# One SBUF tile for all slabs, with slabs 1 and 2 loaded by one DMA and slabs 4 and 5 stored by one DMA

## Chip, cores, metric

One core of one Trainium2 chip. The metric is device time in microseconds of that core; lower is better. Some runs fall over 1.5% above the fastest of the same kernel; these are left out of every ratio.

## The reference

Rotary embedding with split heads, on 16 x 512 x 1024 float32 (33.55 MB in, 33.55 MB out):

```python
x = x.reshape(batch, seq, num_heads, head_dim)       # 16, 512, 16, 64
x1, x2 = x[..., :half_dim], x[..., half_dim:]
rotated = np.concatenate([x1 * cos - x2 * sin,
                          x1 * sin + x2 * cos], axis=-1)
```

## The kernel before

The input is cut into eight slabs of two batch entries. A slab is 4 MB: 128 partitions with one row of 32 KB each. Five slabs are held in SBUF at a time, so load 5 waits until store 0 has landed, load 6 for store 1, load 7 for store 2. Loads are issued from SP, stores from ACT.

```python
slots = 5
slabs = ctx.enter_context(tc.tile_pool(name="slabs", bufs=slots))
xpool = ctx.enter_context(tc.tile_pool(name="xpool", bufs=2))

def dram(t, s, a=0, n=W):
    return bass.AP(tensor=t.tensor, offset=t.offset + s * nb * seq * dim + a,
                   ap=[[W, P], [1, n]])

def load(s):
    slab[s] = slabs.tile([P, W], f32, tag="slab", name="slab")
    return nc.sync.dma_start(out=slab[s], in_=dram(x, s))

load(0)
# ... the cos and sin tables are loaded ...
for s in range(1, slots):
    load(s)
# ... tables spread over 128 partitions by four matmuls ...

# passes: slab 0 in two halves, slabs 1 to 5 whole, slabs 6 and 7 in two halves
cast(passes[0])                               # ScalarE: float32 slab -> bf16 xb
for i, (s, r, n) in enumerate(passes):
    if i + 1 < len(passes):
        cast(passes[i + 1])
    # ... xs, xu: this pass's part of slab[s] and xb[s]; t2: bf16 view of slab[s]
    for t, a in ((t2, rpp * hd), (xu, 0)):    # VectorE: two products
        nc.vector.tensor_mul(out=t, in0=xu, in1=view(tab, ...))
    nc.vector.tensor_add(out=xu, in0=xu, in1=view(t2, ...))   # VectorE: the sum
    nc.scalar.copy(out=xs, in_=xu)            # ScalarE: copy back, bf16 -> float32
    if r + n == rpp:
        nc.scalar.dma_start(out=dram(out_flat, s), in_=slab[s])
        if s + slots < nslabs:
            load(s + slots)
```

The framework inserts all semaphores, and at build time it also orders the instructions of each engine. The source's order is a proposal: in the trace of before, slab 1's cast (L110) stands ahead of both copies of slab 0 (L137), while the source has it between them.

## Time and profile before

| | before |
|---|---|
| time, median of 3 | 162.0 us |
| span of the profiled run | 160.2 us |
| ScalarE busy, VectorE busy | 113.6 us (71%), 108.4 us (68%) |
| DMA: bytes, rate over the span | 67.24 MB, 420 GB/s |

Instructions are named by engine and source line; a bracket gives the idle time before one and what ended it. A q behind an engine's name stands for its sequencer, which issues instructions and DMAs.

### The profile page before, as it was taken

The page shows a single profiled execution, that of the slowest core. Times are in us where ns is not written, and L with a number is a line of the kernel's source. Part 1 is how long each engine was busy: PE and PEld are TensorE (multiplying, and loading weights), DVE is VectorE, ACT ScalarE, POOL GpSimd, SP SyncE. Part 2 cuts the span into 40 slices and gives each one's busy share as a digit, 9 for nine tenths or more (in the row PEclk, how much of TensorE's full clock was granted, in tenths as well). Part 3 has the DMA queues.
Part 4 walks back from the last instruction along what each step waited for, and adds up shares of the span by engine and source line. Part 5 has one row for each costly group of instructions (what it writes and reads, how often), then busy time and mean ns, then how long its engine had stood idle before and what let it go on. Part 6 is the DMA issues. An engine that isn't in the chain of part 4 may idle for free.

```text
span 160.2 us, 157 instructions
## 1 busy us (share of the span) xinstructions
PE 1.2 (1%) x4; PEld 0.5 (0%) x4; DVE 108.4 (68%) x34; ACT 113.6 (71%) x23; POOL 1.8 (1%) x9
## 2 busy tenths in 40 slices
PE   0001100000000000000000000000000000000000
PEld 0000000000000000000000000000000000000000
DVE  0000399999999996997999499939569599900000
ACT  3005939998959899989969995199995999280000
POOL 2000000000000000000000000000000000000000
DMA  7999999999999999999999999999999999999993
GB/s 237 425 401 409 393 458 458 393 425 483 401 393 507 409 393 475 434 401 442 458 409 425 475 409 401 499 409 393 491 425 393 458 450 401 425 475 409 401 499 147
DMA packets 2464, 67.24 MB, mean 420 GB/s; under 512 B 288, under 2 KB 416, under 8 KB 416
## 3 DMA queue, kind: packets, MB, share of 16 engines
q1 hardware_dynamic: 1152, 33.55, 49.3%
q10 hardware_dynamic: 1312, 33.69, 48.8%
HBM read 33.69 MB, written 33.55 MB: 420 GB/s over the span
## 4 chain that ended last, share of the span: by engine, by line
DMA 41%; ACT 21%; DVE 20%; issue 6%; PE 0%; POOLq 0%; POOL 0%; ACTq 0%; DVEq 0%; SPq 0%
DMA out_dram<-slab 19%; DMA slab<-in_x_dram 15%; ACT slab L137 13%; ACT xb L110 8%; DMA cos_sb<-in_cos_dram 7%; DVE xb L131 7%; DVE slab L131 7%; DVE xb L134 6%; DVE tab L101 1%; PE acc L95 0%; POOLq L172 0%; POOL tab L90 0%; ACTq L139 0%; DVEq L131 0%; SPq L62 0%
## 5 line engine op out<-in xcount | busy, mean ns | idle before, releaser
L110 ACT CAST xb<-slab 128x4096 bf16<-128x4096 f32 (+1 forms) x11 | 56.6, 5155 | 23.5 <-DMA slab<-in_x_dram 22.2
L137 ACT CAST slab<-xb 128x4096 f32<-128x4096 bf16 (+1 forms) x11 | 56.6, 5153 | 5.2 <-DVE xb L134 5.2
L131 DVE TENSOR_TENSOR slab<-xb,tab 128x4096 bf16<-128x4096 bf16 (+1 forms) x11 | 35.9, 3260 | 12.8 <-ACT xb L110 12.7
L131 DVE TENSOR_TENSOR xb<-xb,tab 128x4096 bf16<-128x4096 bf16 (+1 forms) x11 | 35.9, 3261 | 0.3
L134 DVE TENSOR_TENSOR xb<-xb,slab 128x4096 bf16<-128x4096 bf16 (+1 forms) x11 | 35.9, 3260 | 0.3
L101 DVE CAST tab<-acc 128x1024 bf16<-128x1024 f32 x1 | 1.2, 1224 | 18.7 <-PE acc L95 18.7
L110 ACT ACT_TABLE_LOAD x1 | 1.3, 1283 | 2.0 <-issue 2.0
L95 PE MATMUL acc<-tab,pick 64*128 64x256 bf16 x4 | 1.2, 392 | 17.5 <-POOL tab L90 17.5
L83 POOL TENSOR_SCALAR_AFFINE_SELECT pick<-pick 64x128 bf16<-64x128 bf16 x2 | 0.5, 287 | 0.1
L90 POOL CAST tab<-cos_sb 64x256 bf16<-64x256 f32 x1 | 0.4, 389 | 10.6 <-DMA cos_sb<-in_cos_dram 10.6
L95 PEld LDWEIGHTS <-pick 64*128 64x128 bf16 x4 | 0.5, 113 | 17.7 <-issue 16.2
L90 POOL CAST tab<-sin_sb 64x256 bf16<-64x256 f32 x1 | 0.4, 394 | 4.9 <-DMA sin_sb<-in_sin_dram 4.9
L80 POOL MEMSET pick<- 64x256 bf16 x1 | 0.3, 305 | 0.3 <-POOLq L158 0.3
L158 POOL MEMSET const-bfloat16-1.0<- 128x1 bf16 x1 | 0.1, 106 | 0.0
L158 POOL MEMSET const-uint8-127<- 128x1 uint8 x1 | 0.1, 106 | 0.0
L158 POOL MEMSET const-float32-0.0<- 128x1 f32 x1 | 0.1, 103 | 0.2 <-issue 0.2
L158 POOL MEMSET const-float32-1.0<- 128x1 f32 x1 | 0.1, 103 | 0.0
## 6 DMA issues: line engine op xcount, KB each, us to landing
slab<-in_x_dram SPq DMA_DIRECT2D x8, 4096.0 KB, 24.2
out_dram<-slab ACTq DMA_DIRECT2D x8, 4096.0 KB, 25.6
cos_sb<-in_cos_dram ACTq DMA_DIRECT2D x1, 64.0 KB, 11.5
sin_sb<-in_sin_dram ACTq DMA_DIRECT2D x1, 64.0 KB, 16.2
```

The source lines that it names most:

```text
L80: nc.gpsimd.memset(pick, 0.0)
L83: nc.gpsimd.affine_select(out=part, in_=part, compare_op=mybir.AluOpType.not_equal, fill=1.0 - 2.0 * g, base=0, pattern=[[0, P // SP], [-1 ...
L90: nc.gpsimd.tensor_copy(out=view(tab1, i * TW, (1, TW)), in_=t)
L95: nc.tensor.matmul(view(acc, i * rpp * hd + h * half, (hd, rpp), (1, half)), view(pick, i * h * P, (1, P)), view(tab1, i * TW, (half, rpp) ...
L101: nc.vector.tensor_copy(out=tab, in_=acc)
L110: nc.scalar.copy(out=view(xb[s], r * dim, (1, n * dim)), in_=view(slab[s], r * dim, (1, n * dim)))
L131: nc.vector.tensor_mul(out=t, in0=xu, in1=view(tab, a + r * hd, (hd, n), (0, nh), (1, hd)))
L134: nc.vector.tensor_add(out=xu, in0=xu, in1=view(t2, half, (hd, n * nh), (-half, 2), (1, half)))
L137: nc.scalar.copy(out=xs, in_=xu)
L158: nc = _bacc.Bacc("TRN2", target_bir_lowering=False, num_devices=1)
```

## The change

The intent is fewer and larger DMAs: 18 become 16. A persistent tile of five places replaces the pool. Slab s sits at place (s + 1) % 5, which puts 1 beside 2 and 4 beside 5. No compute operation changes.

```diff
-    slabs = ctx.enter_context(tc.tile_pool(name="slabs", bufs=slots))
+    mem = singles.tile([P, slots * W], f32, tag="mem")
+
+    def at(s):
+        return (s + 1) % slots * W
+
+    def dram(t, s, n):
+        return bass.AP(tensor=t.tensor, offset=t.offset + s * nb * seq * dim,
+                       ap=[[W, P], [nb * seq * dim, n], [1, W]])
+
+    def sbuf(s, n):
+        return view(mem, at(s), (W, n), (1, W))
+
+    def load(s, n=1):
+        nc.sync.dma_start(out=sbuf(s, n), in_=dram(x, s, n))
...
-    for s in range(1, slots):
+    load(1, 2)
+    for s in range(3, slots):
         load(s)
...
-            nc.scalar.dma_start(out=dram(out_flat, s), in_=slab[s])
+            if s != 4:
+                first, count = (4, 2) if s == 5 else (s, 1)
+                nc.scalar.dma_start(out=dram(out_flat, first, count),
+                                    in_=sbuf(first, count))
```

(Cut: the compute lines, where slab[s] becomes a view of mem at at(s).)

More of the change, by code (lines that the diff above doesn't have):

```diff
@@ L44 @@
         name="psum", bufs=1, space=bass.MemoryType.PSUM))
-    def dram(t, s, a=0, n=W):
-        return bass.AP(tensor=t.tensor, offset=t.offset + s * nb * seq * dim + a,
-                       ap=[[W, P], [1, n]])
     def view(t, offset, *dims):
@@ L54, in view @@
                                    ap=[t.ap[0], *[list(d) for d in dims]])
-    slab = {}
-    def load(s):
-        slab[s] = slabs.tile([P, W], f32, tag="slab", name="slab")
-        return nc.sync.dma_start(out=slab[s], in_=dram(x, s))
+    mem = singles.tile([P, slots * W], f32, tag="mem")
[8 more added lines that the diff above has]
+        nc.sync.dma_start(out=sbuf(s, n), in_=dram(x, s, n))
     load(0)
@@ L110, in cast @@
         nc.scalar.copy(out=view(xb[s], r * dim, (1, n * dim)),
-                       in_=view(slab[s], r * dim, (1, n * dim)))
+                       in_=view(mem, at(s) + r * dim, (1, n * dim)))
     passes = []
@@ L125 @@
             cast(passes[i + 1])
-        xs = view(slab[s], r * dim, (1, n * dim))
+        xs = view(mem, at(s) + r * dim, (1, n * dim))
         xu = view(xb[s], r * dim, (1, n * dim))
-        t2 = view(slab[s].bitcast(bf16), 2 * r * dim, (1, n * dim))
+        t2 = view(mem.bitcast(bf16), 2 * (at(s) + r * dim), (1, n * dim))
         for t, a in ((t2, rpp * hd), (xu, 0)):
```

## The prediction

> **What bounds the kernel now.** I read the page first: busy shares, the 40 slices, the queues.
>
> ```profile
> PE 1.2 (1%) x4; PEld 0.5 (0%) x4; DVE 108.4 (68%) x34; ACT 113.6 (71%) x23; POOL 1.8 (1%) x9
> ...
> DMA  7999999999999999999999999999999999999993
> GB/s 237 425 401 409 393 458 458 393 425 483 401 393 507 409 393 475 434 401 442 458 409 425 475 409 401 499 409 393 491 425 393 458 450 401 425 475 409 401 499 147
> DMA packets 2464, 67.24 MB, mean 420 GB/s; under 512 B 288, under 2 KB 416, under 8 KB 416
> ...
> q1 hardware_dynamic: 1152, 33.55, 49.3%
> q10 hardware_dynamic: 1312, 33.69, 48.8%
> ```
>
> No compute engine is above 71%, but the DMA row is 9 from the second slice to the last but one: the 16 DMA engines are the bound. A table by windows shows how full they are in each kind of traffic (loads alone, loads and stores, stores alone):
>
> ```profile
> core 0: us, PE busy (x) PEld busy (x) DVE busy (x) ACT busy (x) POOL busy (x), PEclk, DMA share, GB/s
> 2.00:37.00 35.00, 1.16 (x4) 0.35 (x3) 18.18 (x8) 21.73 (x6) 0.78 (x2) 1.00 0.97 412
> 38.00:120.00 82.00, 0.00 (x0) 0.00 (x0) 70.94 (x19) 72.26 (x12) 0.00 (x0) 1.00 1.01 434
> 125.00:155.00 30.00, 0.00 (x0) 0.00 (x0) 13.76 (x6) 15.79 (x5) 0.00 (x0) 1.00 1.01 435
> ```
>
> The share is 1.01 in the last two. Every byte counts, and 67.24 MB at some 430 GB/s is 156 us; the rest of the 160.2 us is the start before the first byte (about 1.5 us), the small table packets, and the last landing. So the bytes are unchanged by the diff, and the only things that can move the time are the rate and *idle time of the DMA engines*. The rest of this text asks whether the queues ever run dry.
>
> The timeline gives the times at which work is put in the queues:
>
> ```profile
> 23.63 7.02 ACT L110 CAST xb<-slab 128x8192 bf16<-128x8192 f32 x1 [2.80 <-DMA slab<-in_x_dram]
> ...
> 30.56 7.11 ACT L137 CAST slab<-xb 128x4096 f32<-128x4096 bf16 x2
> ...
> 33.44 4.42 DVE L131 TENSOR_TENSOR slab<-xb,tab 128x8192 bf16<-128x8192 bf16 x1
> ...
> 37.70 0.35 ACTq L139 DMA_DIRECT2D out_dram<-slab  x1
> ...
> 53.86 0.34 ACTq L139 DMA_DIRECT2D out_dram<-slab  x1
> ...
> 98.21 0.34 ACTq L139 DMA_DIRECT2D out_dram<-slab  x1
> ...
> 114.15 0.34 ACTq L139 DMA_DIRECT2D out_dram<-slab  x1
> ...
> 144.28 0.34 ACTq L139 DMA_DIRECT2D out_dram<-slab  x1
> ```
>
> Stores 0, 1, 4, 5 and 7 in that order. The reader sees that slab 1 is cast the moment it lands (23.63), before slab 0's copies back at 30.56, and that the VectorE goes straight from slab 0 to slab 1 at 33.44.
>
> **What the Trainium skill says.** "DMA: Bandwidth & Descriptors", section "Why a DMA increments its semaphore by 16 and not by 1": only the full count means that all data landed. So in one DMA of two slabs, slab 1 can't be used before slab 2 is there too. Nothing in the trace of before has such a DMA, so this is the premise. "SBUF — State Buffer", section "The DMA setup-cost knee (why "@ 1 MiB" ≠ asymptote)": a transfer pays about 2 us that doesn't scale with bytes, mostly completion latency; coalescing is advised. The trace differs for queued transfers: 4 MB DMAs behind one another already run at 434 to 435 GB/s, so that latency is hidden here and there is nothing for coalescing to win. "Perfetto Trace Analysis", section "DMA Optimizations": splitting may let work start sooner. This change does the reverse; the trace agrees in that the cast of slab 1 waits for its DMA (2.80 us).
>
> **The change part by part.**
> (1) It removes one load and one store issue. Issues take 0.33 to 0.65 us on their queues, beside transfers; 4 MB still goes in 128 rows of 32 KB. Each DMA has 1152/8 = 144 packets, 128 of data and 16 small ones. Taking 2 x 16 small ones away is worth under 0.1 us.
> (2) The single tile keeps five places of 32 KB a partition: slabs 5, 6, 7 take those of slabs 0, 1, 2 as before, and load 5 still waits for store 0 to land, load 6 for store 1, load 7 for store 2. The compute instructions keep shapes and counts (casts 7.02 us, VectorE 4.42 us): 0.
> (3) Slab 1 comes later. Slab 1 landed at 23.63; another 4.19 MB at 432 GB/s (the rate in 20 to 37 us) is 9.7 us, so slabs 1 and 2 land at 33.3. ACT casts slab 1 then. Store 0 stays bound by the VectorE (the tables arrive late, slab 0 is done at 33.5). In the source, ACT's order is copy back of slab 0's first half, cast of slab 1, copy back of the second half, store 0. I take that as the middle case: cast 33.3 to 40.3, copy to 43.9, store 0 at 43.9 (6 us later). VectorE on slab 1: 40.4 to 53.7 (7 us later than at 33.44); copy back 53.7 to 60.7; store 1 at 60.8 (before 53.86).
> Do the queues run dry before that? Until store 1, the work is loads 0 to 4, the tables and store 0: 5 x 4.19 + 0.13 + 4.19 = 25.30 MB. The trace of before has moved 24.77 MB by 60 us; the remaining 0.53 MB takes 1.2 us, so that work is used up at 61.2. Store 0 ends it and lands about 1.5 us later, so load 5 is issued at 62.5 or so; store 1, issued at 60.8, has bytes 1.0 us later (as load 0: issued 0.74, first packets at about 1.7), at 61.8. Idle: 0.6 us.
> (4) Store 4 is held for slab 5. Before, it sat in the queue from 98.21, but the store queue reached it only near 120: by then loads (33.5 MB) are in, and what is left, 160.2 less 120 at 434 GB/s, is about four stores. In the middle case store 1 at 60.8, 14.35 us per slab (54.24 to 68.59, cast to cast): store 2 at 75.1, store 3 at 89.5, cast of slab 5 to 96.5, VectorE to 109.8, copy 116.8, the double store at 116.9. Walking both queues with half the rate each (9.7 us a slab alone, 19.3 shared), store 2 ends at 99, store 3 at 118. So the double store is there, just, and load 7 runs to about 120 as well. Idle: 0. Afterwards stores 4 to 7 are 38.7 us, and store 7 is needed at about 150, against 144.28 before and some 146 now: 4 us of slack.
> Sum: -0.1 + 0 + 0.6 + 0 = +0.5 us in the middle case.
>
> **The rivals.**
> *A: the scheduler puts both copies back before slab 1's cast.* Then store 0 stays at 37.7, but the cast is 37.2 to 44.2, VectorE to 57.5, store 1 at 64.6. Store 0 lands at 61.0 as before and load 5 has bytes at 62: idle 0.8 us. All later stores are 3.8 us later than in the middle case: store 3 at 93.2, VectorE on slab 5 ends at 113.5, the double store at 120.6 with bytes at 121.6; store 3 ends at 117.4 and load 7 at 119.9. Idle 1.7 more. Sum +2.5: 164.5 us. Speaking for it: ACT is idle and those copies are ready at about the same time as the data.
> *B: the order of before stays, slab 1's cast ahead of both copies.* Cast 33.3 to 40.3, copies to 47.4, store 0 at 47.5, cast of slab 2, copy, store 1 at 61.7, bytes at 62.7: idle 1.5 us, the double store at 117.8 in time. 163.5 us. For it: the trace of before has this order; against it: it was chosen when slab 1 came 10 us earlier.
> *C: the larger DMA runs faster, and hides its own delay.* 420 to 435 GB/s over the span, say 3%, would give 157 us. Against: the windows already show 1.01 and 434, and rows and packets keep their size.
> *D: all is hidden; the DMA engines never idle.* 162.0. It takes only that slab 1's delay be 1 us less than I think.
> *E: the single tile makes waits between slabs that don't overlap.* A load of one place waiting on work in another would cost 5 us or more. Against: in the trace of before, the matmuls read one half of a tile at 12.73 while its other half is written at 17.59, so waits go by region.
>
> **Range and chances.** Middle 162.5, A 164.5, B 163.5, D 162.0. With 0.3, 0.25, 0.25, 0.2 the mean is 163.1; I predict 163.1 us. The 8 in 10 range is 161.8 to 165.2: below it lies a gain that the full DMA row denies, above it a tail of A with a wider gap or of E. 2% up is 165.2, 2% down 158.8: faster 0.01, within 2% 0.89, slower 0.10.
>
> **What would show it.** In the changed kernel the first cast of slab 1 should wait for its load until about 33.3, the VectorE show a new wait of 7 to 11 us there, store 1 be issued at 60 to 65, and the DMA row have a dent near 61 us (in case A one more near 120). The rate outside the dents should stay at 430 to 435 GB/s. I am wrong if there is no dent though the time rises (then the two-slab DMA itself is slower), if the time falls under 161 (C), or if a load waits for more than the store of its own place (E).

## More of the kernel before

The groups of waits say who waited for whom: total us, times, longest us. In before, ScalarE waits mostly for loads:

```profile
ACT xb L110 <- DMA slab<-in_x_dram: 22.2, 5, 10.5
...
DVE slab L131 <- ACT xb L110: 12.7, 6, 3.5
...
ACT slab L137 <- DVE xb L134: 5.2, 2, 3.5
```

ScalarE hardly ever waits for VectorE (5.2 us), and the chain that ended last, which follows the last instruction back from releaser to releaser, is mostly transfers:

```profile
DMA 41%; ACT 21%; DVE 20%; issue 6%; PE 0%; POOLq 0%; POOL 0%; ACTq 0%; DVEq 0%; SPq 0%
```

## The result, and the profile after

The changed kernel takes 169.58 us (median of 6 runs, 169.28 to 169.72); before, run beside it, 162.19 us (median of 6, one of them slow; the five fast ones are 161.80 to 162.86). The ratio is 1.0452, interval 1.0424 to 1.0479: slower. Here and below a ratio is the recorded one of fast runs to fast runs of the same rounds, so not quite the ratio of the medians quoted.

The page's DMA row and rates of the changed kernel, and its chain:

```profile
DMA  7999999999999998999699998989855989898985
GB/s 242 390 391 397 476 398 460 406 453 414 453 421 429 445 375 375 445 398 390 265 336 414 421 453 375 492 382 492 382 250 250 499 375 499 375 499 375 499 375 250
...
ACT 38%; DVE 35%; issue 10%; DMA 7%; ACTq 1%; PE 0%; POOLq 0%; POOL 0%; DVEq 0%
```

The bytes are the same 67.24 MB, but the DMA row has holes, and the chain that ended last is now ScalarE and VectorE (38% and 35%) with 7% DMA. Windows laid over the holes, first in the changed kernel (columns: window, its length, busy of PE, PEld, VectorE, ScalarE, POOL, the clock, DMA share, GB/s):

```profile
61.00:62.00 1.00, 0.00 (x0) 0.00 (x0) 1.00 (x1) 0.00 (x0) 0.00 (x0) 1.00 0.08 33
82.00:84.00 2.00, 0.00 (x0) 0.00 (x0) 2.00 (x1) 1.97 (x1) 0.00 (x0) 1.00 0.12 49
85.00:86.00 1.00, 0.00 (x0) 0.00 (x0) 0.97 (x1) 1.00 (x1) 0.00 (x0) 1.00 0.11 33
124.00:127.00 3.00, 0.00 (x0) 0.00 (x0) 3.00 (x2) 2.76 (x1) 0.00 (x0) 1.00 0.00 0
```

and the same windows in before:

```profile
61.00:62.00 1.00, 0.00 (x0) 0.00 (x0) 0.71 (x1) 1.00 (x2) 0.00 (x0) 1.00 1.14 492
82.00:84.00 2.00, 0.00 (x0) 0.00 (x0) 2.00 (x1) 0.53 (x1) 0.00 (x0) 1.00 1.18 508
85.00:86.00 1.00, 0.00 (x0) 0.00 (x0) 1.00 (x1) 1.00 (x1) 0.00 (x0) 1.00 1.14 492
124.00:127.00 3.00, 0.00 (x0) 0.00 (x0) 1.00 (x2) 3.00 (x2) 0.00 (x0) 1.00 1.04 448
```

In these 7 us the changed kernel moves 33 + 2 x 49 + 33 + 0 = 164 KB, where 434 GB/s would have moved 3,038 KB. The 2,874 KB that are missing are 6.6 us at that rate, of the 7.7 us by which the span grew (160.2 to 167.9). So most of the loss is queues that ran empty, and not slower transfers. The rest shows between the holes: from 62 to 80 us the DMA share is 1.00, but 406 GB/s are moved, against 435 in before.

Why they ran empty is in the timeline of the changed kernel (L120 is the cast, L141 the products, L144 the sum, L147 the copy back, L152 a store):

```profile
37.52 0.35 ACTq L152 DMA_DIRECT2D out_dram<-mem  x1
37.91 13.94 ACT L120 CAST xb<-mem 128x8192 bf16<-128x8192 f32 x2 [0.42 <-ACT mem L147]
44.96 4.42 DVE L141 TENSOR_TENSOR mem<-xb,tab 128x8192 bf16<-128x8192 bf16 x1 [11.16 <-ACT xb L120]
49.42 4.42 DVE L141 TENSOR_TENSOR xb<-xb,tab 128x8192 bf16<-128x8192 bf16 x1
53.76 4.42 DVE L141 TENSOR_TENSOR mem<-xb,tab 128x8192 bf16<-128x8192 bf16 x1
58.09 4.42 DVE L144 TENSOR_TENSOR xb<-xb,mem 128x8192 bf16<-128x8192 bf16 x1
...
62.60 7.02 ACT L147 CAST mem<-xb 128x8192 f32<-128x8192 bf16 x1 [10.76 <-DVE xb L144]
...
69.65 0.34 ACTq L152 DMA_DIRECT2D out_dram<-mem  x1
...
126.79 0.39 ACTq L152 DMA_DIRECT2D out_dram<-mem  x1
...
155.02 0.34 ACTq L152 DMA_DIRECT2D out_dram<-mem  x1
```

Three things are to be seen. ScalarE now finishes slab 0 (copies, store 0 at 37.52) before it casts slab 1, at 37.91 instead of 23.63, and then casts slabs 1 and 2 in a row. VectorE idles 11.16 us, then works slab 1's two products (44.96, 49.42), *slab 2's first product* (53.76), and only then slab 1's sum (58.09). So ScalarE idles 10.76 us for that sum, and store 1 leaves at 69.65 instead of 53.86. The groups of waits say the same in totals:

```profile
ACT mem L147 <- DVE xb L144: 26.9, 5, 10.8
DVE mem L141 <- ACT xb L120: 23.9, 5, 11.2
```

From 5.2 to 26.9 us and from 12.7 to 23.9 us: the two engines now wait for one another.

### The profile page after: what moved, and what is told of

It reads as the page before. It is cut to its first block, busy times and chain, and to the rows that moved or that the text cites. A ratio compares the mean times of both kernels' runs of the same rounds, so it can differ in the third digit from the quotient of the medians.

```text
span 167.9 us, 154 instructions
## 1 busy us (share of the span) xinstructions
PE 1.2 (1%) x4; PEld 0.4 (0%) x4; DVE 107.8 (64%) x34; ACT 113.7 (68%) x23; POOL 1.8 (1%) x9
## 2 busy tenths in 40 slices
DMA packets 2432, 67.24 MB, mean 400 GB/s; under 512 B 256, under 2 KB 384, under 8 KB 384
## 3 DMA queue, kind: packets, MB, share of 16 engines
q1 hardware_dynamic: 1136, 33.55, 47.9%
HBM read 33.69 MB, written 33.55 MB: 400 GB/s over the span
## 4 chain that ended last, share of the span: by engine, by line
ACT 38%; DVE 35%; issue 10%; DMA 7%; ACTq 1%; PE 0%; POOLq 0%; POOL 0%; DVEq 0%
ACT mem L147 21%; ACT xb L120 17%; DVE mem L141 15%; DVE xb L141 12%; DVE xb L144 8%; DMA cos_sb<-in_cos_dram 7%; ACTq L152 1%; DVE tab L111 1%; PE acc L105 0%; POOLq L186 0%; POOL tab L100 0%; ACTq L147 0%; DVEq L141 0%
## 5 line engine op out<-in xcount | busy, mean ns | idle before, releaser
L147 ACT CAST mem<-xb 128x4096 f32<-128x4096 bf16 (+1 forms) x11 | 56.7, 5155 | 26.9 <-DVE xb L144 26.9
L120 ACT CAST xb<-mem 128x4096 bf16<-128x4096 f32 (+1 forms) x11 | 56.4, 5154 | 12.4 <-DMA mem<-in_x_dram 10.7
L141 DVE TENSOR_TENSOR mem<-xb,tab 128x4096 bf16<-128x4096 bf16 (+1 forms) x11 | 35.8, 3259 | 24.1 <-ACT xb L120 23.9
L144 DVE TENSOR_TENSOR xb<-xb,mem 128x4096 bf16<-128x4096 bf16 (+1 forms) x11 | 35.8, 3259 | 0.2
L141 DVE TENSOR_TENSOR xb<-xb,tab 128x4096 bf16<-128x4096 bf16 (+1 forms) x11 | 35.8, 3259 | 0.2
```

Of the source, the lines that this page charges most:

```text
L120: nc.scalar.copy(out=view(xb[s], r * dim, (1, n * dim)), in_=view(mem, at(s) + r * dim, (1, n * dim)))
L141: nc.vector.tensor_mul(out=t, in0=xu, in1=view(tab, a + r * hd, (hd, n), (0, nh), (1, hd)))
L144: nc.vector.tensor_add(out=xu, in0=xu, in1=view(t2, half, (hd, n * nh), (-half, 2), (1, half)))
```

## The experiments

Theories at the start: (T1) slab 1 comes late because it shares a DMA with slab 2, which delays the stores until the queues run dry; the held store 4 adds to it. (R1) A two-slab DMA is slower by itself. (R2) The single tile makes waits between places that don't overlap. (R3) The held store 4 is most of it. Later T1 split in two: does the data's lateness cost the time (T1a), or the instruction order that was built for it (T1b)? All ten runs gave correct results, and all were timed in 3 rounds against before, on its chip.

| run | slabs 1, 2 loaded | stores 4, 5 | instruction order | us (median) | ratio |
|---|---|---|---|---|---|
| changed kernel | together | together | as built | 169.58 | 1.045 |
| e1_tile_only | apart | apart | as built (that of before) | 162.19 | 1.000 |
| e2_load_pair_only | together | apart | as built | 168.17 | 1.037 |
| e3_store_pair_only | apart | together | as built | 161.99 | 1.000 |
| e4_swap_loads | apart, 2 first | apart | as built (that of e2) | 168.63 | 1.040 |
| e5_dve_order | together | together | VectorE: source's | 165.58 | 1.021 |
| e6_both_orders | together | together | both: source's | 163.88 | 1.010 |
| e7_pair_2_3 | apart (2, 3 together) | together | as built | 164.3 (2 fast runs) | 1.013 |
| e8_load_pair_dve_order | together | apart | VectorE: source's | 164.44 | 1.015 |
| e9_late_order_early_data | apart | apart | that of e2, forced | 168.19 | 1.040 |
| e10_early_order_late_data | together | apart | that of before, forced | 165.10 | 1.018 |

At a threshold of 2%, the changed kernel, e2, e4 and e9 are slower, e5 and e10 unclear (their intervals cross 2%), and the others the same. Smaller differences below are read from the intervals.

### Which part costs

**e1_tile_only**: the tile alone.

```diff
-    load(1, 2)
-    for s in range(3, slots):
+    for s in range(1, slots):
         load(s)
...
-            if s != 4:
-                first, count = (4, 2) if s == 5 else (s, 1)
-                nc.scalar.dma_start(out=dram(out_flat, first, count),
-                                    in_=sbuf(first, count))
+            nc.scalar.dma_start(out=dram(out_flat, s, 1), in_=sbuf(s, 1))
```

> One persistent tile, but every slab loaded and stored by its own DMA. My theory (slab 1 arrives late because it shares a DMA with slab 2): same time as before, 162.2 us, ratio 1.00, no dent in the DMA row. Rival 'the single tile makes waits between slabs that do not overlap': 165 us or more, with a load waiting for more than the store of its own place.

Measured 162.19 us, ratio 1.0002 (0.9985 to 1.002). R2 is out.

**e2_load_pair_only**: e1 with `load(1, 2)` kept.

> Slabs 1 and 2 loaded by one DMA, slabs 4 and 5 stored by two. My theory: the two early dents of the changed kernel (about 61 and 82 to 88 us, some 4.8 us together from rates of 384 and 191 GB/s against 430) stay and the late one (122 to 128 us, 2.4 us) is gone: 166.5 us, store 1 again at about 69.7. Rival 'the held store 4 costs most of it': 163 us or less.

Measured 168.17 us, ratio 1.0369 (1.0348 to 1.0391). The load pair alone makes most of the loss, so R3 is out. The number was missed by 1.7 us: I had taken away the last hole and nothing else, but with store 4 in time the end is set by store 7, issued at 154.42, when the store queue is already empty. Two lines of this run's trace show it:

```profile
154.42 0.34 ACTq L149 DMA_DIRECT2D out_dram<-mem  x1
...
154.00:155.00 1.00, 0.00 (x0) 0.00 (x0) 0.00 (x0) 0.39 (x1) 0.00 (x0) 1.00 0.08 33
```

**e3_store_pair_only**: e1 with the store pair kept.

> Slabs 4 and 5 stored by one DMA, slabs 1 and 2 loaded by two. My theory: the double store is issued at about 117.8, before the store queue has finished store 3 near 119, so nothing runs dry: 162.2 to 163 us. Rival 'holding store 4 costs 2.4 us by itself' or 'a two-slab store is slower': 164.6 us.

Measured 161.99 us, ratio 1.0003 (0.9961 to 1.0046). The double store left at 117.61, and a window from 116 to 122 us shows a DMA share of 1.00 and 431 GB/s: no hole. A held store was free here, while the queue was full. It costs where the stores are late already: 169.58 less 168.17, 1.4 us, beside e2.

**e4_swap_loads**: e1 with two loads changing places, no two-slab DMA anywhere.

```diff
-    for s in range(1, slots):
+    for s in (2, 1, 3, 4):
         load(s)
```

> No two-slab DMA at all; only the loads of slabs 1 and 2 change places in the queue, so that slab 1 lands last of the two, at about 33.5 us. My theory: the same time as the run with the load pair alone, within 0.5 us (166.5), store 1 at about 69.7. Rival 'the two-slab DMA itself is slower': 162.2 to 163 us here.

Measured 168.63 us, ratio 1.0400 (1.0361 to 1.0439): the time of e2 within 0.5 us (its own number, 166.5, was missed as in e2). R1 is out as the cause of the loss: the loss is there without any larger DMA. A listing of the instructions of each engine showed one thing more: e4 was built with the same order on ScalarE and VectorE as e2, e1 with that of before. So slab 1 later in the load queue was enough to change the order.

### Lateness or order

The order can be forced by chaining instructions at build time. This is meant to add no wait on the chip for another engine, only to fix the issue order on one. The control for that is e9 below: with e2's order forced, it has the same two long waits as e2, built without the chain (VectorE 11.16 us, ScalarE 10.76 us).

```diff
+    def after(key, ins):          # each instruction behind the last of its chain
+        ins = ins.ins
+        if key in last:
+            tc.add_manual_dep(ins, last[key].name,
+                mybir.DependencyInfo(mybir.DependencyClass.NoSync,
+                                     mybir.DependencyReason.DATA), reason="order")
+        last[key] = ins
...
-            nc.vector.tensor_mul(...)
+            after('dve', nc.vector.tensor_mul(...))
-        nc.vector.tensor_add(...)
+        after('dve', nc.vector.tensor_add(...))
```

**e5_dve_order**: this on the changed kernel, VectorE only.

> The changed kernel with both two-slab DMAs, but the VectorE held to the source's order (slab 1's three operations before slab 2's first). Theory (lateness of slab 1, then the interleaved order on the VectorE, then the held store 4): store 1 at about 65.3 instead of 69.65 and store 7 at about 148 instead of 155; the dent at 82 to 88 us goes, the one before the double store stays (up to 4 us): 166 to 167 us. Rival 'the order does not matter, the two-slab load alone does it': 169.6 us.

Measured 165.58 us, ratio 1.0212 (1.0181 to 1.0242), a little below what was expected; store 1 at 65.22, store 7 at 147.77, both as expected. The interleaved VectorE order was worth 4.0 us (169.58 less 165.58), and 3.7 us on e2 (168.17 less 164.44, e8 below). The chain also undid the interleaving of the halves of slabs 0 and 6; store 0 left at 37.30, hardly sooner than the 37.52 of the changed kernel. The hole at 82 to 88 us is gone, as expected (437 GB/s there). The hole before the double store (issued at 123.07) is there, shorter than my 4 us: the DMA share is 0.31 from 122 to 124 us.

**e8_load_pair_dve_order**: the same chain on e2.

> The two-slab load alone (stores 4 and 5 apart) with the VectorE held to the source's order. Theory: store 1 at about 65.3, store 7 at about 148 to 150, a dent of about 1 us at 61 us: 163.2 to 164.2 us, so that with the run that adds the double store the held store 4 shows as about 3 us. Rival 'store 4 is never the bound': the same as that run.

Measured 164.44 us, ratio 1.0152 (1.0105 to 1.0199); 0.2 us above the expected band; store 1 at 65.61, store 7 at 150.52. Beside e5 the held store 4 is 1.1 us, not the 3 that I expected, and the two intervals overlap slightly, so even that is not clear of the noise.

**e6_both_orders**: the changed kernel, casts and copies chained too, in the source's order.

```diff
-        nc.scalar.copy(out=view(xb[s], ...), in_=view(mem, ...))
+        after('act', nc.scalar.copy(out=view(xb[s], ...), in_=view(mem, ...)))
...
-        nc.scalar.copy(out=xs, in_=xu)
+        after('act', nc.scalar.copy(out=xs, in_=xu))
```

> The changed kernel with both two-slab DMAs, VectorE and ScalarE held to the source's order, so that slab 1 is cast between the two copies back of slab 0 and slab 2 only after store 0. This is the middle case of my prediction. Theory: store 1 at about 61, double store at about 117.5, store 7 near 146, a dent of 0.6 to 1.3 us at 61 us only: 163 to 163.5 us. Rival 'the late data alone costs it, in any order': 167 us or more.

Measured 163.88 us, ratio 1.0101 (1.0069 to 1.0133), 0.4 us above the expected band. This is the middle case of the prediction, on the chip: store 1 at 61.03 (predicted 60.8), double store at 118.73 (116.9), store 7 at 147.09 (some 146). Both two-slab DMAs are in it, and 5.7 us of the 7.4 (169.58 less 162.19) are gone. The small hole is about where it was foreseen: 66 GB/s from 62 to 63 us, worth some 0.85 us, against 0.6 predicted. But this is less than half of the 2.0 us by which the span is longer than before's (162.2 and 160.2). The first line below is from the timeline, the second a window behind the start of the hole, the third the same window in before:

```profile
33.55 7.02 ACT L134 CAST xb<-mem 128x8192 bf16<-128x8192 f32 x1 [2.73 <-DMA mem<-in_x_dram]
...
62.00:80.00 18.00, 0.00 (x0) 0.00 (x0) 16.64 (x5) 17.59 (x3) 0.00 (x0) 1.00 0.98 382
...
62.00:80.00 18.00, 0.00 (x0) 0.00 (x0) 16.92 (x4) 17.59 (x3) 0.00 (x0) 1.00 1.01 435
```

The first line also gives the landing of the two-slab load: 33.55. The windows show what the prediction had no term for: for 18 us the DMA engines are busy (0.98), hole included, yet 53 GB/s less is moved, 2.2 us' worth. From 80 us to the end the rate is 433 GB/s. All of e2, e4, e5, e8, e9, e10 and the changed kernel have such a stretch (share 0.96 to 1.04 at 379 to 408 GB/s in the same 18 us); before, e1 and e3, without a hole, do not (431 to 435). Why busy engines move less there stays open.

**e9_late_order_early_data**: e1's DMAs, one per slab and slab 1 first, but ScalarE and VectorE chained to exactly e2's order (compared instruction by instruction). The edit traces the passes in that order and chains both engines; its core is

```diff
+    early = {0: 1, 2: 3}          # this pass's sum after that pass's first product
+    cast_at = {1: ([], [2])}      # slab 1's cast behind slab 0's copies and store
...
+        if i not in early.values():
+            mul(i, True)
+        mul(i, False)
+        if i in early:
+            mul(early[i], True)
+        after('dve', nc.vector.tensor_add(...))
```

> No two-slab DMA: every slab has its own, slab 1 lands at about 23.6 us as before. But ScalarE and VectorE are held to exactly the instruction order of the run with the load pair alone (copies of slab 0 and its store, then the casts of slabs 1 and 2; slab 2's first product before slab 1's sum). Theory now: the order costs it, not the data's arrival, since slab 1's cast started at 37.8 there though the data lay ready from about 33.5: 168 us within 0.5, store 1 at about 69.5. Rival 'the late data costs it': 162.2 to 163.5.

Measured 168.19 us, ratio 1.0398 (1.0353 to 1.0443); store 1 at 69.10:

```profile
37.36 13.94 ACT L133 CAST xb<-mem 128x8192 bf16<-128x8192 f32 x2 [0.42 <-ACT mem L175]
...
53.21 4.42 DVE L161 TENSOR_TENSOR mem<-xb,tab 128x8192 bf16<-128x8192 bf16 x1
...
69.10 0.34 ACTq L177 DMA_DIRECT2D out_dram<-mem  x1
```

Slabs 1 and 2 are cast in a row from 37.36, behind slab 0's copies, and slab 2's first product is at 53.21, as in the changed kernel. **With the data early and no merged DMA at all, the order alone gives e2's time.** T1b is shown; that the data's lateness matters *in that order* (T1a) is refuted.

**e10_early_order_late_data**: the reverse. e2's DMAs, with both engines chained to exactly before's order (`early = {0: 1}`, slab 1's cast ahead of slab 0's copies).

> The two-slab load of slabs 1 and 2 (stores 4 and 5 apart), with ScalarE and VectorE held to exactly the instruction order of the kernel before (slab 1's cast ahead of both copies of slab 0, VectorE slab by slab). My prediction's case B. Theory: cast of slab 1 at 33.5, store 0 at 47.7, store 1 at about 62, a dent of about 2 us near 62 us: 163.5 to 164.5. Rival 'the late data costs it, in any order': 168.

Measured 165.10 us, ratio 1.0181 (1.0154 to 1.0208), 0.6 us above the expected band. ScalarE stands waiting in front of a cast whose data is late, with finished work behind it:

```profile
33.16 7.02 ACT L134 CAST xb<-mem 128x8192 bf16<-128x8192 f32 x1 [12.55 <-DMA mem<-in_x_dram]
...
47.22 0.35 ACTq L178 DMA_DIRECT2D out_dram<-mem  x1
...
61.00:62.00 1.00, 0.00 (x0) 0.00 (x0) 1.00 (x1) 0.59 (x2) 0.00 (x0) 1.00 0.01 0
```

(The first two are from its timeline, the last from a window.) The copies of slab 0 follow only at 40.08, and store 0 leaves at 47.22 instead of 37.70. The four corners, with two stores for slabs 4 and 5 throughout:

| | order of before | order of e2 |
|---|---|---|
| slab 1 lands by itself | 162.19 (e1) | 168.19 (e9) |
| slab 1 lands with slab 2 | 165.10 (e10) | 168.17 (e2) |

Lateness costs 2.9 us in the order of before and nothing in the order of e2, where ScalarE reaches slab 1's cast only at 37.8, four microseconds after the data. The order costs 6.0 us with early data. The two don't add up: each has the same effect, a late store 1 (61.58 in e10, 69.10 in e9, 53.86 in before).

### Is a two-slab load harmless elsewhere?

**e7_pair_2_3**: the pair is moved one slab on.

```diff
-    load(1, 2)
-    for s in range(3, slots):
-        load(s)
+    load(1)
+    load(2, 2)
+    load(4)
```

> The same two-slab store, and a two-slab load of slabs 2 and 3 instead of 1 and 2, no order forced. Slab 2 then lands at about 43.3, 5 us after ScalarE wants it, slab 3 still before it is wanted (54.2). Theory: store 1 stays at 53.9, the queues never run dry, 162.2 to 162.7 us. Rival 'a two-slab load costs some us wherever it is': 165 us or more.

Two of the four runs are 163.95 and 164.62 us, ratio 1.0130 (1.0083 to 1.0176). My expectation missed by about 1.5 us. Slab 2 landed at 45.59, not 43.3 (the load shares the engines with store 0 from 37.76 on), and ScalarE, in order, waits for it while slab 1's copy back is held behind:

```profile
45.59 7.02 ACT L120 CAST xb<-mem 128x8192 bf16<-128x8192 f32 x1 [7.85 <-DMA mem<-in_x_dram]
...
59.55 0.34 ACTq L152 DMA_DIRECT2D out_dram<-mem  x1
```

Store 1 leaves at 59.55 instead of 53.86. So neither of the two pairs tried was free, though this one stayed under 2%. Not all of e7's loss need be its load: it has the two-slab store too, which left at 120.86, and from 118 to 124 us 322 GB/s are moved, against 437 in before. No run separates the two. No version beat before, and none of these edits could be expected to: its DMA share is 0.97 to 1.01 in the three windows of the prediction, so an order has nothing to win there.

## Why the prediction was wrong

Predicted were 163.1 us, 161.8 to 165.2, with 0.10 for over 2% slower; measured were 169.58.

**What held.** The bound (the DMA engines) and the question (do the queues run dry) are as predicted, and so is the place of one hole (near 61). Case A also had one before the double store, near 120; it came at 124 to 127. The hole at 82 to 88 us stood in no case. The tile of part 2 costs nothing (e1), but part 2 also put the compute at 0 because shapes and counts stay: its order did not stay. The rate of 430 to 435 GB/s outside the dents held in part only (406 GB/s from 62 to 80 us at a DMA share of 1.00; see e6). Rivals C, D and E are refuted (169.58 us; e1). The landing of slabs 1 and 2 was put at 33.3, and was 33.55 in e6.

**The step that failed is part 3,** "I take that as the middle case: cast 33.3 to 40.3, copy to 43.9". Two of the prediction's own signs show it: slab 1's cast never waited for its load (it started at 37.91, 0.42 us behind a copy), and store 1 left at 69.65, not at 60 to 65. The build chose case A's order on ScalarE (copies and store 0 first; 37.52 in the trace, 37.7 in case A). Case A had been given a quarter, and its sum was too small mostly by one thing that no case contained: all assumed that VectorE does a slab's three operations in a row. It did slab 2's first product before slab 1's sum. That is 4.42 us on slab 1, and 4.0 us of the time by e5. In e5, which is case A without that interleaving, the chip took 165.58 against case A's 164.5: that far the working was sound. The middle case as such measured 163.88 (e6) against 162.5, and case B 165.10 (e10, without the double store that case B has) against 163.5; so the walks of the queues were each 1.1 to 1.6 us too hopeful as well. They counted idle time alone. In e6 the idle time is close to what they gave; the remainder lies behind the hole, where the engines are busy and move less.

**Part 4 was mis-sized with it.** The double store was put at 116.9 with 0 us idle, or at 120.6 in case A. It left at 126.79, after 3 us of empty queues. By itself it costs nothing (e3), beside the late stores 1.4 us (changed kernel less e2; 1.1 for e5 less e8, not clear of noise), because without it store 7's late issue sets the end anyway.

**What the profile of before had shown.** The hint stood in its timeline, in VectorE's operations on the two halves of slab 0:

```profile
24.51 2.28 DVE L131 TENSOR_TENSOR slab<-xb,tab 128x4096 bf16<-128x4096 bf16 x1
26.71 2.28 DVE L134 TENSOR_TENSOR xb<-xb,slab 128x4096 bf16<-128x4096 bf16 x1
```

The second half's first product (24.51) comes before the first half's sum (26.71). With the merged load the same thing happens to slabs 1 and 2, at twice the size. *Why* the build decides so can't be seen in a trace. That its choice follows the expected order of arrival is an inference, from e4 (slab 1 later, nothing merged: e2's order) and e1 (before's order). It is not the whole rule: in e7 slabs 2 and 3 land together, and VectorE still works slab by slab, in e3's order.

## What to carry to other kernels

Where a build step orders the instructions, a change of a transfer is also a change of the program: compare the order on every engine before explaining a time by the transfer. Coalescing queued transfers that already ran at the full rate won nothing here, while the first consumer could start only after the last byte (2.9 us in an unchanged order, e10 less e1). In a kernel bound by its transfers, look at when work enters the queues: a store held back was free while the queue was full (e3) and cost 1.4 us where it wasn't.

## What the Trainium skill lacked or had wrong

- "SBUF — State Buffer", section "The DMA setup-cost knee (why "@ 1 MiB" ≠ asymptote)" advises to coalesce into the largest single transfer. It lacks the case of transfers queued behind one another: 4 MB DMAs ran at 434 to 435 GB/s, merging two of them gained nothing (e3: 161.99 us against 162.19 for e1). Where the first half was wanted early, merging cost 2.9 us in an unchanged instruction order (e10: 165.10) and 6.0 us with the order that was then built (e2: 168.17).
- "DMA: Bandwidth & Descriptors", section "Where 436 GB/s comes from", says that for transfers between HBM and SBUF the HBM side, about 358 GB/s, binds. The section lacks the condition that the same page states under its measured table: that figure is each core's share when both cores of a memory domain stream. With this one core running, loads and stores together moved 434 GB/s in 38 to 120 us and stores alone 435.
- No page that I read says that a changed transfer can change the instruction order of a build. Forced alone, without any change of a transfer, that order took 168.19 us against 162.19 (e9, e1).
